# Gate parts requested two steps sooner, a first gate read cut by expert tile, and the last two expert tiles multiplied together

## The chip, the cores and the metric

The kernel runs on one core of a Trainium2 chip. The metric is device time in microseconds (us) of one execution; each version was run several times and the median is what counts.

## The reference

One decoder layer on 512 tokens of 1024 channels: a gated convolution and recurrence mixer, then a product-key expert layer (PEER), then a final norm. The change touches the expert layer and the end only. Cut to what matters there:

```python
q  = (xc @ w_q)                        # 8 heads, two halves
v1, i1 = top_k(s1, 16); v2, i2 = top_k(s2, 16)
top_s, pos = top_k(all pair sums, 16)  # 16 of 128*128 experts per head
g   = softmax(top_s)
act = gelu(sum(u_sel * xc))            # u_sel = expert_u[idx]
out = sum(g * act * v_sel)             # v_sel = expert_v[idx]
h   = h + out
return rms_norm(h, norm_final)
```

## The kernel before

Matrix products are made from a high and a low part of each float32 operand: `split` (lines 72 to 77) writes the high part on ScalarE (ACT, line 75) and the low part on VectorE (DVE) or GpSimd (POOL) (line 76), and three TensorE (PE) matmuls make the product. `weights` (line 79) loads a tile of 512 KB with a DMA on SyncE's queue (SP, line 81) into one of four `raw` buffers and splits it.

The expert layer treats its 512 tokens in two ways. The last 128 are gathered: POOL fetches the chosen experts' rows, DVE multiplies and sums them (`gathered`, line 400). The first 384 (ND, three groups of 128, NT) go through all 128 tiles of 128 experts densely. For this a gate value for each of the 384 tokens and 16384 experts is made by one-hot products (lines 570 to 593), which pass through a staging tile `stg` to a scratch array `gscr` in DRAM: twelve stores of 2 MB, line 593, on ACT's DMA queue. In `gscr` the gates of one expert row, eight tiles (JG) and 32 tokens lie in one piece of 1 KB.

Per tile j, `act_tile` (line 370) multiplies the tokens with the tile's `expert_u` and applies gelu on ACT (line 378). For 76 of the tiles (those in `LAG`) that is done ahead, beside the making of the gates; twelve of them stay on the chip (`keep`), the others are written to `ascr` and read back (`back`, line 674) three steps before use. `out_tile` (line 639) multiplies the activations with the gates on DVE (line 649), splits them into `w_hi` and `w_lo`, and adds three token groups times two column halves into six accumulators `acc` on PE (line 658): 18 matmuls a tile. The loop of line 684 runs one tile ahead: act_tile(j), then out_tile(j-1).

The gates come back from `gscr` in groups of eight tiles, in two buffers `gt`: `read_gates` (line 631). Of each next group four parts, of three token blocks each, are requested in the tiles with k = 3, 4, 5 and 6 of the present group (k = j % 8, lines 645 and 646). The first group is read in six parts of two token blocks at j = 0 (lines 643 and 644). The requests stand on ACT in the order in which the program is written; ACT works through its instructions in order, and a request goes out when ACT comes to it.

At the end, `finish` (line 614) takes each token group's two accumulators: two squares with sums on ACT, an addition, a square root (ACT, line 620), a reciprocal, two multiplications on DVE (line 624), two stores. In the last tile the 18 matmuls go token group by token group, so that the groups become ready one after the other.

Of the kernel before, what the change touches and what calls it, by code (L numbers as in the profile page):

```python
# [11 lines left out]
F32 = mybir.dt.float32  # L12
# [5 lines left out]
AF = mybir.ActivationFunctionType  # L18
# [3 lines left out]
P = 128  # L22
D = 1024
S = 512
# [11 lines left out]
TG = 32  # L36
NG = ND // TG
JG = 8
# [18 lines left out]
def layer(ctx: ExitStack, tc: tile.TileContext, a):  # L57
    nc = tc.nc
    V, A, G, T, SP = nc.vector, nc.scalar, nc.gpsimd, nc.tensor, nc.sync
# [7 lines left out]
    def bank(names, shape=(P, S), dt=F32):  # L67
        i = rot.get(names, 0)
        rot[names] = i + 1
        return ps_pool.tile(list(shape), dt, tag="b" + names[i % len(names)], name="ps")  # L70
# [8 lines left out]
    def weights(src, k, eng=None):  # L79
        raw = ring.tile([P, k * P], F32, tag="raw", name="raw", bufs=4)  # L80
        SP.dma_start(raw, src)
        hi, lo = split(raw, [P, k * P], ("whi", "wlo"), ring, 3, eng)
        return hi.rearrange("p (k m) -> p k m", k=k), lo.rearrange("p (k m) -> p k m", k=k)
# [19 lines left out]
    epst = cst.tile([P, 1], F32, name="epst")  # L103
# [8 lines left out]
    gscr = dram.tile([NG, P, P, TG], F32, name="gscr")  # L112
# [36 lines left out]
    with tc.tile_pool(name="mix", bufs=1) as mp:  # L149
# [9 lines left out]
        for k in range(KD):  # L159
            n = mp.tile([P, S], F32, tag="tmp", name="xg", bufs=3)  # L160
# [8 lines left out]
        for j in range(2, NEARLY):  # L169
            w = weights(a["w_in"][24 + j], KD)  # L170
# [19 lines left out]
        acc = cst.tile([P, KR], F32, name="acc_t")  # L190
# [23 lines left out]
        for j in range(KR):  # L214
# [16 lines left out]
            c = next(columns)  # L231
            held[c] = proj(c, COLS)
            gates = []
            for s, bname, tag in ((0, "brg", "lr"), (1, "big", "lx")):
# [3 lines left out]
                gt = mp.tile([P, S], F32, tag=tag, name=tag, bufs=KR)  # L238
# [88 lines left out]
        for i in range(KD):  # L327
# [4 lines left out]
            n = mp.tile([P, S], F32, tag="tmp", name="hg", bufs=3)  # L332
# [50 lines left out]
    def lag_tiles(n):  # L383
        for _ in range(n):
            j = next(ahead_of_gates, None)
            if j is None:
                return
            kept[j] = act_tile(j)
            if j not in LAG[:JK]:
                A.dma_start(ascr[j], kept[j])  # L390
# [9 lines left out]
    def gathered(i, pin=False):  # L400

        r = gp.tile([P, 2 * D], F32, tag="row", name="row", bufs=4)
        ins = G.indirect_dma_start(  # L403
            out=r, out_offset=None, in_=a["uv"], in_offset=bass.IndirectOffsetOnAxis(ap=uidx[:, i : i + 1], axis=0)
        )
        if pin:
            tc.keep_in_program_order(ins)
        junk = gp.tile([P, D], BF16, tag="junk", name="junk", bufs=1)
        tc.keep_in_program_order(
            V.scalar_tensor_tensor(junk, r[:, :D], 1.0, n2tok, op0=ALU.mult, op1=ALU.mult, accum_out=dots[:, i : i + 1])  # L410
        )
        A.activation(dots[:, i : i + 1], dots[:, i : i + 1], AF.Gelu_apprx_tanh)
        A.activation(dots[:, i : i + 1], dots[:, i : i + 1], AF.Copy, scale=gk[:, i : i + 1])  # L413
        if lastrow:
            gathered_sum()
        lastrow.append((i, r))
# [5 lines left out]
    with tc.tile_pool(name="top", bufs=1) as rp:  # L422
# [77 lines left out]
        for hd in range(H):  # L500
            qs = []
            for s in range(2):
                n = 2 * hd + s
# [48 lines left out]
    with tc.tile_pool(name="gates", bufs=1) as rp:  # L552

        ioR = rp.tile([P, P, 2], F16, name="ioR")
        G.iota(ioR, pattern=[[1, P], [0, 2]], base=0, channel_multiplier=0, allow_small_or_imprecise_dtypes=True)
        TP = TE // 2

        def rows_of(t, t0):
            def bc(x):
                return x[:, t0 : t0 + TE].rearrange("p (q t) -> p q t", t=2).unsqueeze(2).to_broadcast([P, TP, P, 2])  # L560

            e12 = rp.tile([P, 2, TP, P, 2], F16, tag="e12", name="e12", bufs=2)
            ehl = rp.tile([P, 2, TP, P, 2], F16, tag="ehl", name="ehl", bufs=2)
            for s in range(2):
                V.tensor_tensor(e12[:, s], ioR.unsqueeze(1).to_broadcast([P, TP, P, 2]), bc(iT[t][:, s]), op=ALU.is_equal)  # L565
            for s in range(2):
                V.tensor_mul(ehl[:, s], e12[:, 0], bc(gT[t][:, s]))  # L567
            return e12[:, 1], ehl[:, 0], ehl[:, 1]

        blocks = [(t, t0) for t in range(NT) for t0 in range(0, P, TE)]  # L570
        ahead = rows_of(*blocks[0])
        for n, (t, t0) in enumerate(blocks):
            e2, eh, el = ahead
            if n + 1 < len(blocks):
                ahead = rows_of(*blocks[n + 1])
            c, s0 = divmod(t0, TG)
            if s0 == 0:
                stg = rp.tile([P, P, TG], F32, tag="stg", name="stg", bufs=2)
            for q4 in range(TE // 4):
                pg = bank("4567")  # L580
                for i in range(4):
                    o = pg[:, i * P : (i + 1) * P]
                    ti = 4 * q4 + i
                    T.matmul(o, e2[:, ti // 2, :, ti % 2], eh[:, ti // 2, :, ti % 2], start=True, stop=False)
                    T.matmul(o, e2[:, ti // 2, :, ti % 2], el[:, ti // 2, :, ti % 2], start=False, stop=True)
                A.activation(
                    stg[:, :, s0 + 4 * q4 : s0 + 4 * q4 + 4],
                    pg.rearrange("p (t i) -> p i t", t=4),
                    AF.Copy,
                    scale=1.0 / GSC,  # L590
                )
            if s0 + TE == TG:
                A.dma_start(gscr[t * (P // TG) + c], stg)
            left = NL - AR - AD * NT - AT
            lag_tiles((n + 1) * left // len(blocks) - n * left // len(blocks))
            for i in range(n * UP // len(blocks), (n + 1) * UP // len(blocks)):
                gathered(i)
        lag_tiles(AT)


    ep = ctx.enter_context(tc.tile_pool(name="exp", bufs=1))
    gfin = ep.tile([P, D], F32, name="gfin")
    SP.dma_start(gfin, a["nfin"].to_broadcast([P, D]))
    acc = [[ps_pool.tile([P, S], F32, tag=f"b{2 + 2 * t + f}", name=f"acc{t}{f}") for f in range(2)] for t in range(NT)]
    def residual(k):
        hk = ep.tile([P, S], F32, tag="hk", name="hk", bufs=2)
        SP.dma_start(hk, hscr[:, k, :])
        c = (k % 4) * P
        for t in range(NT):
            T.matmul(  # L610
                acc[t][k // 4][:, c : c + P], hk[:, t * P : (t + 1) * P], ident, start=False, stop=False, skip_group_check=True
            )
# [13 lines left out]
                SP.dma_start(a["out"][t * P : (t + 1) * P, fs], o[:, fs])  # L626

    nout = 0
    gst = {}

    def read_gates(n, c0, c1):

        if n * JG >= P:
            return
        if c0 == 0:
            gst[n] = ep.tile([P, NG, JG, TG], F32, tag="gt", name="gt", bufs=2)
        tc.keep_in_program_order(A.dma_start(gst[n][:, c0:c1], gscr[c0:c1, :, n * JG : (n + 1) * JG, :].rearrange("c p j t -> p c j t")))

    def out_tile(j, g):
        nonlocal nout  # L640
        k = j % JG
        if j == 0:
            for c in range(0, NG, 2):
                read_gates(0, c, c + 2)
        if 3 <= k < 7:
            read_gates(j // JG + 1, 3 * k - 9, 3 * k - 6)
        gt = gst[j // JG][:, :, k, :]
        gv = g.rearrange("p (c t) -> p c t", t=TG)
        tc.keep_in_program_order(V.tensor_mul(gv, gv, gt))
        v = weights(a["uv"][j * P : (j + 1) * P, D:], KD, V)  # L650
        vf = [x.rearrange("p k m -> p (k m)") for x in v]
        w = split(g, [P, ND], ("w_hi", "w_lo"), ep, 2)
        passes = [(x, y, f) for x, y in ((0, 0), (0, 1), (1, 0)) for f in range(2)]
        if nout == P - 1:
            passes.sort(key=lambda p: p[2])
        for t in range(NT):
            for x, y, f in passes:
                T.matmul(  # L658
                    acc[t][f],
                    w[x][:, t * P : (t + 1) * P],  # L660
                    vf[y][:, f * S : (f + 1) * S],
                    start=nout == 0 and (x, y) == (0, 0),
                    stop=nout == P - 1 and (x, y) == (1, 0),
                    skip_group_check=True,
                )
        nout += 1

    spilled = list(LAG[JK:])
# [15 lines left out]
    for j in range(P + 1):  # L684
        if j < P:
            read_back(j + PRE)
            g = kept[j] if j in LAG else act_tile(j)
            part += share[j]
        if prev is not None:
            out_tile(*prev)  # L690
        if 8 <= j < 8 + 2 * KD and j % 2 == 0:
            residual(j // 2 - 4)
        prev = (j, g)
        while done < min(len(work), math.ceil(part * len(work) / total)):
            work[done]()
            done += 1
# [54 lines left out]
```

## Time and profile before

| | us |
|---|---|
| median of 3 runs (1783.91 to 1791.77) | 1784.34 |
| the profiled execution, its own time | 1786.26 |
| its span in the profile | 1784.5 |
| PE busy, share of the span | 97% |
| DVE busy, share | 72% |
| ACT busy, share | 43% |

The busy share of PE is an average over stages, and a busy PE is not one at its peak: matmuls are pipelined. More is to be had from the places where PE waits, from the granted clock after such a wait, and from what stands after the last matmul. The dense expert stage, in which PE adds into `acc`, runs from 1011 us to 1776 us.

### The profile page before, as it was taken

To read this page: it belongs to the slowest core of one execution; us is meant where nothing else is said; L and a number is where in the kernel's file an instruction comes from. 1 tells how busy PE (TensorE), PEld (TensorE's weight loads), DVE (VectorE), ACT (ScalarE), POOL (GpSimd) and SP (SyncE) were. 2 spreads that over 40 slices of the span, in tenths; PEclk is the share of its full clock that TensorE was granted. 3 is DMA by queue.
4 is the path that set the end of the run, shared out by engine and by line. 5 is a ranking of instruction groups with operands and counts; after the bars stand their busy time and mean duration, and the time that the engine had idled before them with its cause. 6 is when DMAs were issued, how large, how long until landed. Compare 5 with 4: busy or idle time off the path is not lost.

```text
span 1784.5 us, 23972 instructions
## 1 busy us (share of the span) xinstructions
PE 1728.9 (97%) x8861; PEld 1509.5 (85%) x8861; DVE 1287.8 (72%) x2341; ACT 764.2 (43%) x1290; POOL 325.2 (18%) x257
## 2 busy tenths in 40 slices
PE   7999999999989999899999899999999999999998
PEld 6888888888879888899999788888888887888886
DVE  8979443224578658999998576788777786878774
ACT  5774342222343335455454343444443443444353
POOL 0000000000045555122221121222211222212200
PEclk9999999999999999899999999999999999999999
DMA  4323322332433334579999898999888998999862
GB/s 169 113 81 108 103 77 91 108 102 96 130 112 105 106 113 164 191 275 343 363 368 385 307 332 307 320 339 356 325 297 306 334 339 292 333 338 346 308 237 88
DMA packets 124247, 410.85 MB, mean 230 GB/s; under 512 B 12129, under 2 KB 55393, under 8 KB 106081
## 3 DMA queue, kind: packets, MB, share of 16 engines
q1 hardware_dynamic: 59904, 199.58, 32.8%
q0 software_dynamic: 18432, 134.23, 19.7%
q10 hardware_dynamic: 45792, 75.51, 11.8%
q8 instruction: 69, 1.13, 0.2%
q14 instruction: 50, 0.40, 0.1%
HBM read 367.33 MB, written 41.94 MB: 229 GB/s over the span
## 4 chain that ended last, share of the span: by engine, by line
PE 77%; DVE 11%; DMA 6%; issue 4%; ACT 1%; POOL 1%; SPq 0%; DVEq 0%; POOLq 0%; ACTq 0%
PE ps L90 48%; PE acc L658 26%; DMA gt<-gscr 4%; DVE wlo L76 2%; DVE ehl L567 2%; DVE e L565 1%; DMA row<-uv,uidx 1%; DVE yg L397 1%; DVE junk L410 1%; PE ps L518 1%; PE ps L237 1%; POOL row L403 1%; DMA raw<-ut 1%; DVE nk L142 1%; DMA raw<-w_in 0%
## 5 line engine op out<-in xcount | busy, mean ns | idle before, releaser
L75 ACT ACTIVATE whi<-raw 128x1024 fp32r<-128x1024 f32 (+1 forms) x364 | 380.1, 1046 | 615.0 <-PE ps L90 386.0
L76 DVE TENSOR_TENSOR wlo<-raw,whi 128x1024 fp32r<-128x1024 f32 (+1 forms) x324 | 388.9, 1204 | 263.5 <-ACT whi L75 262.2
L90 PE MATMUL ps<-q_hi,whi 128*128 128x384 f32 (+1 forms) x1232 | 434.4, 353 | 14.9 <-ACT whi L75 10.3
L90 PE MATMUL ps<-q_hi,wlo 128*128 128x384 f32 (+1 forms) x1232 | 429.1, 348 | 2.1 <-DVE wlo L76 2.1
L90 PE MATMUL ps<-q_lo,whi 128*128 128x384 f32 (+1 forms) x1232 | 428.4, 348 | 0.3 <-DVE q_lo L144 0.3
L403 POOL DMA_INDIRECT row<-uv,uidx x128 | 201.4, 1573 | 752.2 <-DVE yg L397 747.6
L658 PE MATMUL acc<-whi,w_hi 128*128 128x512 f32 x768 | 242.4, 396 | 20.6 <-ACT w_hi L75 15.8
L90 PEld LDWEIGHTS ps<-q_hi,whi 128*128 128x128 f32 x1232 | 233.4, 189 | 27.5 <-ACT whi L75 11.6
L90 PEld LDWEIGHTS ps<-q_hi,wlo 128*128 128x128 f32 x1232 | 233.1, 189 | 13.9 <-DVE wlo L76 4.9
L90 PEld LDWEIGHTS ps<-q_lo,whi 128*128 128x128 f32 x1232 | 233.6, 190 | 10.7 <-DVE q_lo L144 0.7
L658 PE MATMUL acc<-wlo,w_hi 128*128 128x512 f32 x768 | 240.7, 394 | 0.0
L658 PE MATMUL acc<-whi,w_lo 128*128 128x512 f32 x768 | 240.7, 394 | 0.0
L658 PEld LDWEIGHTS acc<-whi,w_hi 128*128 128x128 f32 x768 | 145.0, 191 | 50.1 <-ACT w_hi L75 19.0
L658 PEld LDWEIGHTS acc<-whi,w_lo 128*128 128x128 f32 x768 | 146.1, 191 | 31.7 <-DVE w_lo L76 0.7
L658 PEld LDWEIGHTS acc<-wlo,w_hi 128*128 128x128 f32 x768 | 146.0, 190 | 31.5 <-DVE wlo L76 0.3
L90 PE MATMUL ps<-n_hi,whi 128*128 128x512 f32 x432 | 168.5, 390 | 0.0
L90 PE MATMUL ps<-n_hi,wlo 128*128 128x512 f32 x432 | 168.2, 390 | 0.0
L90 PE MATMUL ps<-n_lo,whi 128*128 128x512 f32 x432 | 168.1, 389 | 0.0
L397 DVE SCALAR_TENSOR_TENSOR yg<-row,dots,yg 128x1024 f32<-128x1024 f32 x128 | 164.4, 1284 | 0.8 <-ACT dots L413 0.8
L76 POOL TENSOR_TENSOR wlo<-raw,whi 128x1024 fp32r<-128x1024 f32 x40 | 98.4, 2462 | 357.9 <-ACT whi L75 357.9
L410 DVE SCALAR_TENSOR_TENSOR junk<-row,n2tok 128x1024 bf16<-128x1024 f32 x128 | 156.3, 1221 | 0.2 <-DMA row<-uv,uidx 0.2
L90 PEld LDWEIGHTS ps<-n_hi,wlo 128*128 128x128 f32 x432 | 81.1, 188 | 17.3 <-DVE wlo L76 0.4
(204 smaller groups left out, 1908.1 us busy)
## 6 DMA issues: line engine op xcount, KB each, us to landing
raw<-ut SPq DMA_DIRECT2D x128, 512.0 KB
raw<-uv SPq DMA_DIRECT2D x128, 512.0 KB
raw<-w_in SPq DMA_DIRECT2D x60, 512.0 KB
gscr<-stg ACTq DMA_DIRECT2D x12, 2048.0 KB
gt<-gscr ACTq DMA_DIRECT2D x60, 384.0 KB
ascr<-gel ACTq DMA_DIRECT2D x64, 192.0 KB
back<-ascr ACTq DMA_DIRECT2D x64, 192.0 KB
raw<-w_q SPq DMA_DIRECT2D x16, 512.0 KB
```

The lines of the kernel that those rows point to most:

```text
L75: A.activation(hi, raw, AF.Copy)
L76: (lo_eng or V).tensor_sub(lo, raw, hi.bitcast(F32))
L90: T.matmul(ps, w[x][:, i, :], r[y][i], start=first and n == 0, stop=last and n == 3 * k - 1)
L142: V.scalar_tensor_tensor(n, src[:, k, :], col(gname, k), rstd, op0=ALU.mult, op1=ALU.mult)
L237: T.matmul(pg, x[:, s * P : (s + 1) * P], y, start=n == 0, stop=n == 2)
L397: V.scalar_tensor_tensor(yg, r[:, D:], dots[:, i : i + 1], yg, op0=ALU.mult, op1=ALU.add)
L403: ins = G.indirect_dma_start(out=r, out_offset=None, in_=a["uv"], in_offset=bass.IndirectOffsetOnAxis(ap=uidx[:, i : i + 1], axis=0))
L410: V.scalar_tensor_tensor(junk, r[:, :D], 1.0, n2tok, op0=ALU.mult, op1=ALU.mult, accum_out=dots[:, i : i + 1])
L518: T.matmul(psc[:, s * P : (s + 1) * P], qs[s][:, t * P : (t + 1) * P], keys[:, 2 * hd + s, :], start=True, stop=True)
L565: V.tensor_tensor(e12[:, s], ioR.unsqueeze(1).to_broadcast([P, TP, P, 2]), bc(iT[t][:, s]), op=ALU.is_equal)
L567: V.tensor_mul(ehl[:, s], e12[:, 0], bc(gT[t][:, s]))
L658: T.matmul(acc[t][f], w[x][:, t * P : (t + 1) * P], vf[y][:, f * S : (f + 1) * S], start=nout == 0 and (x, y) == (0, 0), stop=nout == P - ...
```

## The change

Four edits. The four parts of the next group's gates are requested at k = 1 to 4 in place of 3 to 6. The last of the twelve stores is made in two, the first eight tiles' gates and then the rest. The first group's gates are read in three parts cut by tile (0 and 1, 2 and 3, 4 to 7), each over all twelve token blocks, in place of six parts cut by token block. The matmuls of tile 126 are held back until tile 127's operands are there, and then both tiles are multiplied token group by token group; ahead of them a square root on ACT, of which nothing is used, brings the table of that function in.

```diff
             if s0 + TE == TG:
-                A.dma_start(gscr[t * (P // TG) + c], stg)
+
+                for i0, i1 in ((0, P),) if n + 1 < len(blocks) else ((0, JG), (JG, P)):
+                    A.dma_start(gscr[t * (P // TG) + c][:, i0:i1], stg[:, i0:i1])
...
+    operands = []
...
         if j == 0:
-            for c in range(0, NG, 2):
-                read_gates(0, c, c + 2)
-        if 3 <= k < 7:
-            read_gates(j // JG + 1, 3 * k - 9, 3 * k - 6)
+
+            gst[0] = ep.tile([P, NG, JG, TG], F32, tag="gt", name="gt", bufs=2)
+            for j0, j1 in ((0, 2), (2, 4), (4, JG)):
+                tc.keep_in_program_order(
+                    A.dma_start(gst[0][:, :, j0:j1], gscr[:, :, j0:j1, :].rearrange("c p j t -> p c j t"))
+                )
+        if 1 <= k < 5:
+            read_gates(j // JG + 1, 3 * k - 3, 3 * k)
...
-        passes = [(x, y, f) for x, y in ((0, 0), (0, 1), (1, 0)) for f in range(2)]
-        if nout == P - 1:
-            passes.sort(key=lambda p: p[2])
+        operands.append((w, vf))
+        if nout == P - 2:
+            nout += 1
+            return
+
         for t in range(NT):
-            for x, y, f in passes:
-                T.matmul(
...
+            for n, (w, vf) in enumerate(operands):
+                passes = [(x, y, f) for x, y in ((0, 0), (0, 1), (1, 0)) for f in range(2)]
+                last = nout == P - 1 and n == 1
+                if last:
+                    passes.sort(key=lambda p: p[2])
+                for x, y, f in passes:
+                    T.matmul(
...
+        operands.clear()
         nout += 1
...
+        if j == P - 1:
+
+            tc.keep_in_program_order(A.activation(ep.tile([P, 1], F32, name="warm"), epst, AF.Sqrt))
```

The first place is ACT ahead of the boundary to the seventh group (tile 48). Names with a number are buffers; `gt<-gscr` is the request for a part of the gates, `gel<-ps` the gelu of an act_tile, `w_hi` the split of an out_tile, and the words in brackets are the semaphores that are waited for (DMAHW is a DMA that has landed). Before, the fourth part stands between the gelu 11755 and its split, and one tile further comes `w_hi_11839`, the first that needs it:

```order
L378 ACTIVATE gel_11755<-ps_11730 128x384 [waits PE_49]
L637 DMA gt_11575<-gscr_78 128x3x256 [waits DMAHW1_49]
L75 ACTIVATE w_hi_11803<-gel_11755 128x384 [waits DVE_49]
L75 ACTIVATE whi_11865<-raw_11863 128x1024 [waits DMAHW5_49,PE_49]
L412 ACTIVATE dots_3822<-dots_3822 128x1 [waits DVE_49]
L413 ACTIVATE dots_3822<-dots_3822,gk_3821 128x1 [waits Activation_49]
L75 ACTIVATE w_hi_11839<-back_11613 128x384 [waits DMAHW6_49,DVE_49]
```

With the change the same group's fourth part stands here, two tiles ahead of that place:

```order
L378 ACTIVATE gel_11646<-ps_11621 128x384 [waits PE_49]
L640 DMA gt_11506<-gscr_78 128x3x256 [waits DMAHW3_49]
L75 ACTIVATE w_hi_11694<-gel_11646 128x384 [waits DVE_49]
L75 ACTIVATE w_hi_11763<-back_11544 128x384 [waits DMAHW0_49,DVE_49,PE_49]
L75 ACTIVATE whi_11759<-raw_11757 128x1024 [waits DMAHW7_49,PE_49]
```

The request has moved ahead by two tiles' work of ACT; in this group it stands where the third part stood. The three earlier parts have moved with it, and all behind it on ACT keeps its order.

The second place is DVE at the start of the stage, with the change. `keep_3983` is tile 0, `keep_4016` tile 2 and `gel_9403` tile 1:

```order
L656 TENSOR_TENSOR keep_3983<-keep_3983,gt_9405 128x384 [waits DMAHW4_49,DMAHW3_49]
L656 TENSOR_TENSOR keep_4016<-keep_4016,gt_9405 128x384 [waits DMAHW5_49]
L76 TENSOR_TENSOR w_lo_9417<-keep_3983,w_hi_9416 128x384 [waits Activation_49]
L410 SCALAR_TENSOR_TENSOR junk_9440,dots_3822<-row_9438,n2tok_3823 128x1024 [waits DMASW1_49]
L397 SCALAR_TENSOR_TENSOR yg_3824<-row_9365,dots_3822,yg_3824 128x1024
L656 TENSOR_TENSOR gel_9403<-gel_9403,gt_9405 128x384 [waits DMAHW4_49,DMAHW2_49]
```

The order of these is that of before, where the first multiplication waited for all six parts. Now each waits for its own part, and the multiplication of tile 2, with the second part, stands ahead of the low half of tile 0.

The third place is the end of ACT. Before:

```order
L75 ACTIVATE w_hi_15730<-gel_15692 128x384 [waits DVE_49]
L75 ACTIVATE w_hi_15759<-back_15568 128x384 [waits DMAHW3_49,DVE_49,PE_49]
L617 ACTIVATE fo_15781,fss_15783<-acc00_9358 128x512 [waits PE_49]
L617 ACTIVATE fo_15781,fss_15783<-acc01_9359 128x512 [waits PE_49]
L617 ACTIVATE fo_15781,fss_15794<-acc10_9360 128x512 [waits PE_49]
L620 ACT_TABLE_LOAD
L620 ACTIVATE fs1_15786<-fs1_15786,epst_70 128x1 [waits DVE_49]
```

And with the change:

```order
L75 ACTIVATE w_hi_15728<-gel_15690 128x384 [waits DVE_49]
L710 ACT_TABLE_LOAD
L710 ACTIVATE warm_15732<-epst_70 128x1
L75 ACTIVATE w_hi_15741<-back_15566 128x384 [waits DMAHW1_49,DVE_49,PE_49]
L619 ACTIVATE fo_15781,fss_15783<-acc00_9359 128x512 [waits PE_49]
L619 ACTIVATE fo_15781,fss_15783<-acc01_9360 128x512 [waits PE_49]
L622 ACTIVATE fs1_15786<-fs1_15786,epst_70 128x1 [waits DVE_49]
```

The table load has moved ahead of the last tile's split, and each token group's square root now follows its own two squares.

## Rows read from the trace of the kernel before

**Rows 1.** The page, part 4: lines in the chain that ended last.

```profile
PE ps L90 48%; PE acc L658 26%; DMA gt<-gscr 4%; DVE wlo L76 2%; DVE ehl L567 2%; DVE e L565 1%; DMA row<-uv,uidx 1%; DVE yg L397 1%; DVE junk L410 1%; PE ps L518 1%; PE ps L237 1%; POOL row L403 1%; DMA raw<-ut 1%; DVE nk L142 1%; DMA raw<-w_in 0%
```

**Rows 2.** Waits, 1011 us on (us, times, longest); tile gt, idle until.

```profile
PE acc L658 <- ACT w_hi L75: 15.8, 7, 3.7
...
ACT w_hi L75 <- DMA raw<-uv: 0.5, 1, 0.5
...
  DMA gt<-gscr: 34.6, 8
```

**Rows 3.** The chain in order of time: start us, us, what and how many.

```profile
1105.14 6.12 PE acc L658 x18
...
1115.42 4.09 PE acc L658 x18
...
1285.97 9.66 DMA gt<-gscr
1296.82 6.03 PE acc L658 x18
...
1354.72 10.10 PE acc L658 x36
...
1491.74 6.00 PE acc L658 x18
...
1547.38 8.47 PE acc L658 x36
...
1593.83 4.38 PE acc L658 x18
...
1683.76 5.79 PE acc L658 x18
```

**Rows 4.** Windows: length, PE, PEld, DVE, ACT, POOL busy, clock, DMA share, GB/s.

```profile
1296.00:1302.50 6.50, 5.68 (x18) 4.37 (x19) 6.50 (x10) 2.23 (x4) 0.00 (x0) 0.74 0.81 257
1106.00:1286.00 180.00, 180.00 (x870) 158.19 (x869) 143.84 (x185) 75.96 (x140) 41.91 (x27) 0.99 0.91 332
1300.00:1740.00 440.00, 429.46 (x2032) 373.79 (x2032) 336.98 (x435) 185.14 (x335) 84.08 (x58) 0.99 0.87 313
```

**Rows 5.** Timeline, boundary to the seventh group: ACT's requests, then DVE's multiplication.

```profile
1269.98 0.62 ACTq L637 DMA_DIRECT2D gt<-gscr  x1
...
1285.97 0.37 ACTq L637 DMA_DIRECT2D gt<-gscr  x1
...
1295.65 0.56 DVE L649 TENSOR_TENSOR back<-back,gt 128x384 f32<-128x384 f32 x1 [3.58 <-DMA gt<-gscr]
```

**Rows 6.** Start of the stage: ACT, DVE, PE; SP's wait; packets 1003.2:1010, 688:690.5.

```profile
1000.17 0.92 ACTq L637 DMA_DIRECT2D gt<-gscr  x2
...
1010.14 1.03 DVE L649 TENSOR_TENSOR keep<-keep,gt 128x384 f32<-128x384 f32 x2 [1.45 <-DMA gt<-gscr]
...
1011.35 1.19 PE L658 MATMUL acc<-whi,w_hi 128*128 128x512 f32 x2 [4.84 <-issue]
...
SPq L603 <- DMA gscr<-stg: 12.3, 1, 12.3
...
q10 hardware_dynamic: 1632, 1.57, 68.6%
...
q1 hardware_dynamic: 288, 0.13, 19.1%
```

**Rows 7.** The end: PE's last matmul (timeline), then the chain.

```profile
1775.54 0.39 PE L658 MATMUL acc<-whi,w_lo 128*128 128x512 f32 x1
...
1772.56 2.05 ACT fo L617 x6
...
1774.63 1.28 ACT L620
...
1776.22 1.73 ACT fo L617 x6
...
1778.49 1.41 DVE fo L624 x2
```

More of the change, by code (lines that the diff above doesn't have):

```diff
@@ L652, in out_tile @@
         w = split(g, [P, ND], ("w_hi", "w_lo"), ep, 2)
-        passes = [(x, y, f) for x, y in ((0, 0), (0, 1), (1, 0)) for f in range(2)]
-        if nout == P - 1:
-            passes.sort(key=lambda p: p[2])
+        operands.append((w, vf))
+        if nout == P - 2:
+            nout += 1
+            return
         for t in range(NT):
-            for x, y, f in passes:
-                T.matmul(
[L659 to L665, printed above, removed]
+            for n, (w, vf) in enumerate(operands):
[5 more added lines that the diff above has]
+                    T.matmul(
+                        acc[t][f],
+                        w[x][:, t * P : (t + 1) * P],
+                        vf[y][:, f * S : (f + 1) * S],
+                        start=nout == 0 and (x, y) == (0, 0),
+                        stop=last and (x, y) == (1, 0),
+                        skip_group_check=True,
+                    )
+        operands.clear()
         nout += 1
```

## The prediction

> **What bounds the kernel now.** The view to begin with is the chain that ended last. PE leads it, with one stranger of weight: the landing of gate parts, 4% of the span, some 71 us [rows 1]. That share is no gain yet, since PE works through most of each landing. So next come PE's waits from 1011 us on: seven waits for `w_hi`, 15.8 us in all, and almost none of ACT for weights, 0.5 us [rows 2]. `w_hi` is made from the gated activations, and the rows of tile `gt` say what those waited for: DVE stood idle eight times, 34.6 us in all, until gate parts landed [rows 2]. One of the eight is the first group's (below), seven are boundaries between groups.
>
> The timeline at one of them shows why. The second part of four is requested at 1269.98, the fourth at 1285.97, and DVE begins the multiplication at 1295.65, having stood for 3.58 us [rows 5]. A part needs 9.7 us from request to landing, and the fourth is asked for too late by less than that.
>
> Then the price of such a wait, which is more than the wait. In the chain 18 matmuls of a tile take 4.09 us, but 6.12, 6.03 and 6.00 us right after a gap [rows 3]. The window at 1296 has a granted clock of 0.74, against 0.99 in the long stretches [rows 4]: for part of it TensorE ran at 1.2 in place of 2.4 GHz, after PE had stood still.
>
> Is something else ready to take PE's place? In the 180 us from 1106 on there is no gap: PE is busy 180.00 of 180.00, with DMA at 0.91, DVE at 144 and ACT at 76 us [rows 4]. PE sets the pace there. From 1300 to 1740 DMA is at 0.87 and PE lacks 10.5 us [rows 4].
>
> **Part 1, requests two steps sooner.** Removed: the waits at seven boundaries. Idle time, 15.8 us. Slow matmuls, each against 4.09 us for 18 or 8.18 for 36 [rows 3]: 2.03 (1105), 1.94 (1296), 1.92 (1354), 1.91 (1491), 0.29 (1547), 0.29 (1593) and 1.70 (1683), 10.1 us together. Sum 25.9 us. Does two steps suffice? The fourth part now goes out where the second did, in the example 16.0 us sooner, 1269.98 against 1285.97 [rows 5]; DVE's longest wait behind ACT's late request is a few us (34.6 over eight [rows 2]). So none should be left. Added: nothing; the sixty part requests are the same ones, of the same size, at 0.4 to 0.6 us each on ACT's queue. Each reuses the buffer of the group before the present one, whose last multiplication stands two tiles earlier; the order shows no wait of these requests for DVE, only for earlier DMAs, as before. On ACT's DMA queue they pass some `back` reads, which have three steps of lead. With the boundaries gone the same bytes move in 26 us less: 0.87 of 440 is 383 us of DMA work, over some 425 that is 0.90, still under the 0.91 that a gapless stretch carried [rows 4]. I take all of it: **-25.9 us**; bounds 13 (half of the gaps refilled by the next late operand) and 26.
>
> **Part 2, the start.** The store first. SP waited 12.3 us for the last 2 MB store to land, with the weight loads behind it [rows 6]; the tile that SP loads there takes over memory of the staging tile, so it needs both pieces, and the cut doesn't shorten this. The first reads go out at 1000.17, when ACT gets to them, well after that landing. So the store's cut is worth nothing; its second request costs ACT 0.3 us, hidden by ACT's idle half. Then the reads. From the first request to DVE's multiplication 9.97 us pass (1000.17 to 1010.14), and PE stands 4.84 us until 1011.35 [rows 6]. Of the 9.97 the packets themselves take 68.6% of 6.8 us, 4.7 us: 1632 packets over 16 engines, 46 ns each, nearly all of 1 KB. The other 5.3 us are request, queue and weight loads between. The new parts have runs of 256, 256 and 512 bytes, 1536 of them in each part. No row has 256 bytes. The nearest is the stretch at 688: 288 packets, all but 32 of them of 512 bytes, in 19.1% of 2.5 us, 27 ns each [rows 6]. From 46 to 27 ns for half the bytes: the line leads to 18 ns for 256 (an estimate), and 27 is the upper bound by these rows. DVE's second multiplication needs the second part and stands ahead of tile 0's low half, so two parts count: 3072 packets, 3.5 us at 18 ns, 5.2 at 27. With the 5.3 that is 8.8 to 10.5 against 9.97: 1.2 us sooner to 0.5 later. PE gains a bit beside: the first part alone takes 1.7 us, so `w_hi` of tile 0 comes some 3 us sooner, and four matmuls (0.9 us) run before `w_lo` is wanted. I take 18 ns, since the two measured sizes lie on a line: **-2.0 us**, bounds -4 (a wait short enough spares the slow matmuls too) and +1.5.
>
> The Trainium skill ("DMA: Bandwidth & Descriptors", Specifications) has a rule that speaks against this cut: the least transfer for full rate is 512 bytes, and below that the engine reads, modifies and writes. By it part 2 would be the loss of rival (b), and the sum -26 us in place of -30; no row here has such a transfer.
>
> **Part 3, the end.** Before, after the last matmul (1775.93) ACT has ahead of it, the table load having just ended (1774.63 + 1.28): three squares (1.73 us), square roots, then on DVE token group 1's two multiplications (1.41 us) and group 2's [rows 7]. With the change group 0 is complete 24 matmuls (at 4.09 / 18 = 0.23 us each, 5.5 us) and group 1 twelve (2.7 us) before the end, in place of twelve and six; the load is out of the way, and only group 2 is left: one square, 0.68 us (three take 2.05 [rows 7]), an addition, a root, a reciprocal, 1.41 us. Saved: 1.73 - 0.68 = 1.05, one root of 0.3, and 1.41, together 2.8 us. Given back: the load and the idle root stand ahead of the last `w_hi`, which PE now wants six matmuls after tile 126's first; by the timeline's spacing PE may stand 0.2 us, and the addition shows again, 0.2. **-2.3 us**, bounds -1 and -3.
>
> **Sum.** -25.9 - 2.0 - 2.3 = -30.2 us. On the profiled execution's own time, 1786.26, that is 1756; the median of the runs, 1784.34, stands 1.9 lower, so **1754 us**.
>
> **Rivals.** (a) *The weight loads come late.* PE's gaps were also time in which loads caught up; at closed boundaries the next operand is late and half of the 26 us stays. For it: DMA at 0.87 to 0.91, and four more parts in the same few tiles. Against: the gapless 180 us at 0.91, and 0.5 us of waits for weights. Time: 1754 + 13 = 1767. (b) *Small packets cost double*, 36 ns where the line gives 18. Then 3072 of them take 6.9 us, 12.2 us pass in place of 9.97, and the start loses 2 us where I gain 2: 1758. Against: the fall from 46 to 27 ns at half the size. The Trainium skill's rule named in part 2 would bring this about. (c) *Nothing moves*: ACT reaches the earlier requests late, because it stands behind PE's gelu anyhow: 1784. Against: the order has them two tiles ahead, and the second part's time in rows 5. (d) *Slower: ACT stands at the requests.* A request waits for an earlier DMA on its semaphore; two steps sooner that DMA may not have landed, and everything behind on ACT, `whi` and `w_hi`, is late. ACT is busy 76 of 180 us, free 58%, 3.5 us of a 6 us tile. If one request of each of 15 groups stood for a whole landing, 9.7 us, PE would lose 15 x 6.2 = 93 us: about 1847. It outweighs the gain from 2 us over the free time, so from 5.5 us a group. Against: requests at k = 3 to 6 had the same kind of wait, and PE shows none for it.
>
> **Chances.** The forecast 0.75, (a) 0.11, (b) 0.08, (c) 0.03, (d) 0.03. The forecast's own bounds are 1748 to 1763; (b) lies in them, (a) ends at 1767: range **1748 to 1767**, which leaves out part of (a), (c) and (d) and the ends of the bounds. About 0.5% (9 us) is what a measurement of this kernel can tell from no change. Faster by more: forecast, (a) and (b), 0.94. Same: (c), 0.03. Slower: (d), 0.03.
>
> **What would show it.** Right: PE's row for waits on `w_hi` near zero; no idle time of DVE until `gt` beyond the first; a granted clock of 0.99 or 1.0 through the stage; the first `acc` matmul some 3 us sooner, then a short stop; PE's last matmul about 28 us earlier; 6.4 us in place of 8.6 from its end to the end of the span. Wrong: waits of ACT for `raw` (a), the first parts landing after 1010 (b), requests still landing at the boundaries (c), ACT idle at its requests (d).

## The result and the profile after

The changed kernel takes 1755.15 us in the median (four runs, 1753.01 to 1755.78), the kernel before 1784.21 beside it: ratio 0.9824, 95% interval 0.9802 to 0.9846 (it is formed from the runs; the quotient of the two medians is 0.9837). By the medians that is 29.1 us less where 30.2 were forecast; the interval is 27.5 to 35.3 us. Measured again, it took 1756.16 against 1786.56 (ratio 0.9824, 0.9805 to 0.9843), 30.4 us less. The profiled execution took 1753.01 us, its span is 1751.3.

The page's chain, which answers to [rows 1]. The landing of gate parts, 4% before, is no longer in it:

```profile
PE ps L90 49%; PE acc L672 30%; DVE ehl L567 2%; DVE wlo L76 1%; DVE e L565 1%; DMA row<-uv,uidx 1%; PE ps L518 1%; DVE yg L397 1%; DVE junk L410 1%; PE ps L237 1%; DMA gscr<-stg 1%; POOL row L403 1%; DMA raw<-ut 1%; DVE nk L142 1%; DMA raw<-uv 0%
```

Tile `gt` in the trace after, for [rows 2]: DVE's idle time until gate parts landed was 34.6 us in eight stops. Both stops that are left belong to the first group:

```profile
L650 ACTq DMA_DIRECT2D gt<-gscr x3: 380/1129/3538, 999.4 to 1001.0; - x3
...
  DMA gt<-gscr: 5.1, 2
```

PE's waits from 1005 to 1747 us, where before there were 15.8 us for `w_hi`: the answer has its heading and no row. The windows after, for [rows 4] (columns as there):

```profile
1016.00:1747.00 731.00, 729.18 (x3518) 638.62 (x3516) 572.37 (x744) 315.99 (x575) 145.88 (x99) 1.00 0.88 319
1300.00:1740.00 440.00, 440.00 (x2114) 385.69 (x2113) 340.72 (x441) 191.79 (x343) 83.08 (x56) 1.00 0.86 311
1106.00:1286.00 180.00, 180.00 (x872) 157.78 (x871) 142.69 (x184) 77.05 (x141) 40.08 (x26) 1.00 0.92 336
1003.00:1017.00 14.00, 13.85 (x58) 11.45 (x57) 10.24 (x16) 5.58 (x11) 2.02 (x2) 0.90 1.09 304
```

From 1300 to 1740 PE is busy all of 440.00 us, against 429.46, at a granted clock of 1.00. The 180 us that had no gap before are as they were (872 matmuls against 870). The fourth row holds the only stretch in which PE still works at a lower clock, the start of the stage (0.90).

At the boundary to the seventh group, for [rows 5], the timeline has the fourth part's request and DVE's first multiplication with it, 18.4 us later (9.7 before) and without a bracket, so DVE didn't stand for it. The request has moved by 12.3 us and not by the 16.0 of the prediction's example: it stands where the third part stood, as the order ahead of the prediction has it, and the timeline of before has that part, the first line here, at 1273.64, ahead of the fourth at 1285.97. The chain there, for [rows 3], has no tile of over 4.1 us (36 `acc` matmuls, two tiles, in 8.17); it is the third fence.

```profile
1273.64 0.38 ACTq L637 DMA_DIRECT2D gt<-gscr  x1
```

```profile
1264.43 0.38 ACTq L640 DMA_DIRECT2D gt<-gscr  x1
...
1282.78 0.55 DVE L656 TENSOR_TENSOR back<-back,gt 128x384 f32<-128x384 f32 x1
```

```profile
1288.97 4.16 PE ps L90 x24
1293.13 8.17 PE acc L672 x36
1301.30 4.16 PE ps L90 x24
```

The start, for [rows 6], from the timelines of PE, ACT and DVE:

```profile
999.43 1.54 ACTq L650 DMA_DIRECT2D gt<-gscr  x2
...
1000.43 0.44 PE L90 MATMUL ps<-q_hi,whi 128*128 128x384 f32 x1 [2.36 <-ACT whi L75]
...
1001.01 3.54 ACTq L650 DMA_DIRECT2D gt<-gscr  x1
...
1005.58 0.56 DVE L656 TENSOR_TENSOR keep<-keep,gt 128x384 f32<-128x384 f32 x1 [3.95 <-DMA gt<-gscr]
...
1007.17 0.62 PE L672 MATMUL acc<-whi,w_hi 128*128 128x512 f32 x2
1007.32 0.56 DVE L656 TENSOR_TENSOR keep<-keep,gt 128x384 f32<-128x384 f32 x1 [1.18 <-DMA gt<-gscr]
1007.79 0.55 DVE L76 TENSOR_TENSOR w_lo<-keep,w_hi 128x384 fp32r<-128x384 f32 x1
```

From the first request to the first multiplication 6.15 us pass (9.97 before), and the first `acc` matmul follows PE's earlier work with no stop, where it stood 4.84 us. It comes 4.2 us sooner, of which 0.7 are this execution's own: it reached the first request that much earlier (999.43 against 1000.17).

The end, for [rows 7]: PE's last matmul, ACT's table load, which now lies 8.8 us ahead of it, and the last two multiplications:

```profile
1735.97 1.28 ACT L710 ACT_TABLE_LOAD   x1
...
1744.79 0.39 PE L672 MATMUL acc<-whi,w_lo 128*128 128x512 f32 x1
...
1746.66 1.41 DVE L626 SCALAR_TENSOR_TENSOR fo<-acc,fs,gfin 128x512 f32<-128x512 f32 x2
```

From the last matmul's end (1745.18) to the end of the span 6.12 us are left, against 8.57.

### The profile page after: what moved, and what is told of

Its sections match the earlier page's. It is cut to its first block, busy times and chain, and to the rows that moved or that the text cites. A ratio compares the mean times of both kernels' runs of the same rounds, so it can differ in the third digit from the quotient of the medians.

```text
span 1751.3 us, 23967 instructions
## 1 busy us (share of the span) xinstructions
PE 1719.4 (98%) x8861; PEld 1505.5 (86%) x8861; DVE 1287.3 (74%) x2341; ACT 764.2 (44%) x1291; POOL 326.9 (19%) x257
## 3 DMA queue, kind: packets, MB, share of 16 engines
q8 instruction: 69, 1.13, 0.3%
## 4 chain that ended last, share of the span: by engine, by line
PE 81%; DVE 10%; issue 4%; DMA 3%; ACT 1%; POOL 1%; SPq 0%; DVEq 0%; ACTq 0%; POOLq 0%
PE ps L90 49%; PE acc L672 30%; DVE ehl L567 2%; DVE wlo L76 1%; DVE e L565 1%; DMA row<-uv,uidx 1%; PE ps L518 1%; DVE yg L397 1%; DVE junk L410 1%; PE ps L237 1%; DMA gscr<-stg 1%; POOL row L403 1%; DMA raw<-ut 1%; DVE nk L142 1%; DMA raw<-uv 0%
## 5 line engine op out<-in xcount | busy, mean ns | idle before, releaser
L672 PE MATMUL acc<-whi,w_hi 128*128 128x512 f32 x768 | 238.1, 391 | 0.0
```

What stands on the lines that cost most here:

```text
L672: T.matmul(acc[t][f], w[x][:, t * P : (t + 1) * P], vf[y][:, f * S : (f + 1) * S], start=nout == 0 and (x, y) == (0, 0), stop=last and (x, ...
```

## Experiments

Each is the kernel before, or the changed one, with one edit. Differences are of medians, from the kernel before as measured beside each: 1784.88 us under the first heading, 1785.99 under the next two, 1786.56 under the last.

**When the parts are requested**

The requests alone, put into the kernel before:

```diff
-        if 3 <= k < 7:
-            read_gates(j // JG + 1, 3 * k - 9, 3 * k - 6)
+        if 1 <= k < 5:
+            read_gates(j // JG + 1, 3 * k - 3, 3 * k - 0)
```

> The kernel before with one edit: the four parts are requested at k = 1 to 4. My term for this edit is -25.9 us: 1784.2 - 25.9 = 1758. PE's row for waits on w_hi falls from 15.8 us in seven waits to near zero, and no window of the stage after its start has a granted clock under 0.99. Rival 1, the weight loads or another operand are late in the place of the gates and half of the gaps stays: 1771, with a new row of PE or ACT waits of about 13 us. Rival 2, the gain of the whole change came in good part from its other edits (the trace of the changed kernel reaches the stage about 4 us sooner): then this edit gives 20 us or less, 1764 or more.

1761.8 us, 23.1 less (ratio 0.9869, 0.9840 to 0.9899). From 1016 us on PE waits for nothing. The windows from there to the last matmul, of the kernel before and of this one:

```profile
1016.00:1776.00 760.00, 744.17 (x3539) 647.87 (x3538) 571.86 (x738) 315.42 (x570) 144.98 (x99) 0.99 0.85 307
```

```profile
1016.00:1750.00 734.00, 734.00 (x3541) 643.36 (x3540) 571.01 (x738) 314.36 (x569) 146.80 (x99) 1.00 0.87 317
```

The two rows split the gain. Idle time: 760 - 744.17 = 15.8 us. Matmul time: 744.17 / 3539 = 210.3 ns each against 734.00 / 3541 = 207.3, times 3540 is 10.6 us. Together 26 us, the term of 25.9. The profiled executions as a whole agree: 1760.62 against 1786.26, 25.6 less. The medians show 23.1, with an interval of 18.0 to 28.6 us, and can't tell this from 25.9. Of its gain this execution gave a little back in its start: from 1003 to 1017 its granted clock was 0.65, where that of before was 0.88:

```profile
1003.00:1017.00 14.00, 10.16 (x32) 8.59 (x31) 7.86 (x12) 2.98 (x6) 1.01 (x1) 0.65 0.83 266
```

```profile
1003.00:1017.00 14.00, 9.16 (x40) 7.75 (x39) 7.38 (x12) 3.25 (x7) 1.01 (x1) 0.88 0.66 215
```

The first fence is the requests alone, the second the kernel before: eight matmuls fewer in the same 14 us, though PE was busy 1 us more; at 207 ns each that is some 1.7 us. Rival 1 falls, since no new wait came. Rival 2, 20 us or less, falls by the profiled execution's 25.6 and by the next run, in which the other edits alone bring 4.25; the interval of the medians, which begins at 18.0, would not exclude it.

The changed kernel with the requests put back (`if 3 <= k < 7` again):

> The changed kernel with the requests put back to k = 3 to 6, so that only the start and the end are changed. My terms are -2.0 for the start and -2.3 for the end: 1784.2 - 4.3 = 1780, and the seven waits at the boundaries are there again, about 16 us of idle time and about 10 us of matmuls at half the clock. Rival, the start is worth more than I said, since the profile of the changed kernel has its first acc matmul 4.2 us sooner and no slow acc matmul there: 1778 or below. If this kernel and the one with the requests alone do not add up to the whole change (-29.1), the edits are not independent.

1780.63 us (ten runs), 4.25 less than before (0.9978, 0.9962 to 0.9994, which is 1.1 to 6.8 us), the two terms' 4.3. PE's waits for `w_hi` are back, 15.6 us in nine. With the requests alone this makes 27.4 of the whole 29.1 to 30.4: within what these medians can tell, the edits add up.

One step in place of two (`if 2 <= k < 6`), and one step later than before (`if 4 <= k < 8`, in the kernel before):

> The changed kernel with the requests one step sooner than before in place of two, at k = 2 to 5. One step is one tile, 4.1 us of acc matmuls and 4.2 more where the tile's act matmuls lie beside it. DVE's idle time at a boundary was 4.7 us in the mean and PE's 2.3, so my theory expects one step to remove nearly all of PE's waits: at most one or two short ones of under 2 us, 1755 to 1759. Rival, a part lands late because the DMA engines are full and not because it is asked for late: then one step brings half of the gain at most, 1768 or more.

> The kernel before with the requests one step later, at k = 4 to 7. If the lateness of the request sets the wait, the fourth part now goes out in the tile just ahead of the boundary: all 15 boundaries wait, the seven of before for 2.3 + 5.7 = 8 us of PE's time each, the other eight for about 3, which is 80 us in place of 16, and each of the 15 gives about 2 us of slow matmuls, 30 in place of 10: 1784 + 84 = 1868. Rival, PE's queue of finished operands absorbs one step, and only the seven boundaries grow: 7 x 5.7 = 40 us more, 1824. Rival, the landing is set by the DMA load alone: within 10 us of before.

One step sooner gives 1755.44, 29.4 less: all of the gain, so the rival that full DMA engines, and not the request, make the parts late falls. PE's waits from 1006 us on are one, in the start:

```profile
PE acc L672 <- DVE w_lo L76: 1.7, 1, 1.7
```

One step later gives 1825.29, 40.4 more (1.0226, 1.0193 to 1.0260). Its waits, and its window over the stage:

```profile
PE acc L658 <- ACT w_hi L75: 45.2, 12, 7.7
```

```profile
1016.00:1816.00 800.00, 754.78 (x3535) 655.09 (x3534) 572.50 (x739) 315.40 (x569) 140.55 (x100) 0.97 0.82 292
```

Idle time rose by 29.4 us (45.2 against 15.8), matmuls by 754.78 / 3535 - 210.3 = 3.2 ns each, 11 us: 41 in all. So the request's lateness sets the wait, and a wait carries its slow matmuls with it, as the first theory says; but its 84 us was twice too much. The rival's 1824 hit the time by another way than it gave: there are twelve waits, 3.8 us in the mean, at eleven boundaries and not at seven (one boundary has two of them). Why the other four boundaries still don't wait was not tried.

**The start**

The last store in one piece, and the first group read in six parts by token block:

```diff
-                for i0, i1 in ((0, P),) if n + 1 < len(blocks) else ((0, JG), (JG, P)):
-                    A.dma_start(gscr[t * (P // TG) + c][:, i0:i1], stg[:, i0:i1])
+                A.dma_start(gscr[t * (P // TG) + c], stg)
```

> The changed kernel with its last 2 MB store in one piece again. My term for the cut is 0: 1755 within 1.5, with SP's wait for the landing of the store (12.8 us with the cut) as long as there, and the first read's requests at about 999.4 on ACT, when ACT gets to them. Rival, the cut lets the first reads or SP's loads begin sooner: without it the first multiplication of the stage (1005.6 with the cut) is 2 us or more later and the time 1757 or more.

```diff
-            gst[0] = ep.tile([P, NG, JG, TG], F32, tag="gt", name="gt", bufs=2)
-            for j0, j1 in ((0, 2), (2, 4), (4, JG)):
...
+            for c in range(0, NG, 2):
+                read_gates(0, c, c + 2)
```

> The changed kernel with the first group's gates read in six parts by token block, as before. My term for the cut by tile is 2.0 us: 1757, PE with a stop of about 4.8 us ahead of its first acc matmul and slow matmuls behind it. Rival, the cut by tile is worth the whole 4.2 us by which the first acc matmul came sooner, and the half-clock matmuls that follow the long stop besides: 1759 to 1761. Rival by the price of short packets: if packets of 256 bytes were bad, this kernel would be the faster one, 1755 or less.

One store: 1755.91 us, 30.1 less, the same as with two. SP's wait for the landing is 13.1 us (12.8 in two pieces), so the cut is worth nothing. Six parts: 1759.11 us, 26.9 less, where the changed kernel has 29.1 and 30.4, 29.7 in the mean: the cut by tile is worth about 2.8 us, between the term of 2.0 and the rival's 4.2 and more. The interval of this run is 21 to 34 us less, so the medians don't decide between the two; that short packets are bad, with 1755 or less for this kernel, is refuted, its four runs being 1758.38 and more. The stops of PE tell more. For gates and `w_lo` of the first tiles PE stood 4.84, 3.84, 3.31 and 3.31 us in the four profiles with six parts (before, the requests alone, one step later, and this one), 3.8 in the mean. In seven with the cut by tile (the changed kernel, without the requests, one step, one store, the two of the end below, and the changed kernel again) it stood 0, 3.7, 1.7, 1.7, 0.7, 3.1 and 3.1 us, 2.0 in the mean: 1.8 less. The stop in this run:

```profile
1016.22 1.19 PE L669 MATMUL acc<-whi,w_hi 128*128 128x512 f32 x2 [3.31 <-issue]
```

The price of the short packets, from the changed kernel's DMA view of 1002 to 1005 us (queue: packets, MB, share of 16 engines):

```profile
q10 hardware_dynamic: 2431, 0.62, 108.8%
```

0.62 MB over 2431 packets is 255 bytes each; 108.8% of 3 us on 16 engines is 52.2 us, 21 ns a packet (a share of over 100% means that the packets' times overlap). The prediction took 18, with 27 as its upper end.

**The end**

Without the idle square root, and without holding tile 126 back:

```diff
-            tc.keep_in_program_order(A.activation(ep.tile([P, 1], F32, name="warm"), epst, AF.Sqrt))
+            pass
```

> The changed kernel without the idle square root, so that ACT brings the table in at the first group's own square root. The load (1.28 us) then begins when the first group's squares are done, 4.7 us ahead of PE's last matmul, and delays the second group's squares by some 0.4 us, which the pause of 0.8 us ahead of the third group's absorbs: last matmul to end of span 6.1 us as with it, 1755 within 1.5. Rival, the load lies on the path to the end: 1.3 us more, 1756.5, and 7.4 us from the last matmul to the end.

```diff
-        if nout == P - 2:
-            nout += 1
-            return
...
-                last = nout == P - 1 and n == 1
+                last = nout == P - 1
```

> The changed kernel with tile 126 multiplied by itself and tile 127 token group by token group behind it, as before; the idle square root stays. The groups are then ready 2.7 and 1.4 us ahead of the end in place of 5.5 and 2.7. ACT needs 1.35 us for a group's squares and 0.3 for its root, so the second group's squares run past the end of PE by about 1 us: 7.2 us from the last matmul to the end of the span in place of 6.1, 1756.3. Rival, holding the tile back costs PE as much as it gives (a stop ahead of the last two tiles): 1755 or less.

Without the idle root: 1755.64 us, 6.11 us from the last matmul to the end: nothing lost. The timeline of ACT shows the load falling into the pause between two token groups; the third group's squares still had to wait for PE:

```profile
1740.09 1.28 ACT L622 ACT_TABLE_LOAD   x1
...
1744.15 0.60 ACT L619 ACTIVATE fo<-acc 128x512 f32<-128x512 f32 x1 [0.43 <-PE acc L672]
```

Without the hold: 1758.61 us, and 7.35 us after the last matmul (1749.95 of 1757.3), where 7.2 were expected. The tail is thus 8.57 with neither edit, 7.35 with the root alone, 6.11 with the hold alone and 6.12 with both: once the tile is held back, the idle root is worth nothing. The tail explains 1.2 of the 2.3 us by which this kernel's gain, 27.4, is smaller than the changed kernel's 29.7 in the mean; these medians can't place the rest. In this execution PE also stands 1.29 and 1.83 us at the start, but so it does (1.84 and 1.27) in the second profile of the changed kernel.

**More from the start**

In the changed kernel's profile SP's weight loads stand behind `gfin`, whose memory waits for the last store, and PE stands 2.36 us. Four kernels, measured side by side, asked whether that, or the first reads, can give more.

```diff
-    SP.dma_start(gfin, a["nfin"].to_broadcast([P, D]))
...
-        SP.dma_start(hk, hscr[:, k, :])
+        tc.keep_in_program_order(SP.dma_start(hk, hscr[:, k, :]))
...
+        if j == 24:
+            tc.keep_in_program_order(SP.dma_start(gfin, a["nfin"].to_broadcast([P, D])))
```

> The changed kernel with SP's load of the norm weights (gfin) moved from the start of the expert stage to tile 24, and the loads of hk kept in their order behind it, so that SP's weight loads no longer stand behind a tile that waits for the last store. In the profile of the changed kernel PE stands 2.36 and 0.64 us at 1000 us for weights and then runs 3.41 us at half the clock, 1.7 us lost: 4.7 us in all. My theory: the loads go out some 4 us sooner and these go, but the first gates then become late, since ACT comes to their requests only 2 to 3 us sooner; a stop of PE ahead of its first acc matmul of about 2.5 us takes their place: 2 us gained, 1753. Rival 1, the whole 4.7 us are gained: 1750.5. Rival 2, the loads are bounded by the freeing of raw and not by the store: 1755.

> The changed kernel itself, beside the three others of this call, as their measure: 1755 within 1.5.

The changed kernel again: 1756.16 (1751.94 to 1757.04). `gfin` late: 1754.56 (ratios 0.9824 and 0.9820; intervals from 0.9803 to 0.9843 overlap). No wait of SP for the last store is left, but PE's stop for weights is 0.97 us with `gfin` late and also in the second profile of the changed kernel. In six other profiles with this start it is 1.6 to 2.9 us, so one profile of each can't tell what `gfin` gave. What shows is the gates: the second part lands at 1011.65, tile 0's low half stands behind it on DVE, and PE waits there:

```profile
1012.73 1.22 PE L671 MATMUL acc<-whi,w_lo 128*128 128x512 f32 x2 [3.64 <-DVE w_lo L76]
```

So gates do come late in the place of weights, as the theory's later half says, though by 3.64 us where it said 2.5; its price of the loads is not shown. Rival 2, that the loads are bounded by the freeing of `raw`, gave the nearest time, 1755. A gain of 2 us is neither shown nor excluded. The other two write the first requests ahead of the loop; the second also has `gfin` late:

```diff
+    gst[0] = ep.tile([P, NG, JG, TG], F32, tag="gt", name="gt", bufs=2)
+    for j0, j1 in ((0, 2), (2, 4), (4, JG)):
+        tc.keep_in_program_order(
+            A.dma_start(gst[0][:, :, j0:j1], gscr[:, :, j0:j1, :].rearrange("c p j t -> p c j t"))
+        )
```

> The changed kernel with the first group's three requests written ahead of the loop over the tiles, so that on ACT they stand ahead of the first tile's whi and gelu; DVE's order at the start then has tile 0's low half ahead of tile 2's multiplication. SP's loads stay where they are. Theory: the first multiplication comes 2 to 3 us sooner and PE's small stop for w_lo (0.3 to 1.7 us in the runs so far) goes, but the stop of 2.36 + 0.64 us for weights and the half clock after it stay: about 1 us gained, 1754. Rival, the requests wait on ACT for an earlier DMA and hold the work behind them: 1758 or more.

> Both edits: gfin at tile 24 and the first requests ahead of the loop. Theory: neither weights nor gates are late at the start of the stage, PE has no gap of over 1 us between 960 us and its last matmul, and no half-clock window there: 4.7 us of weights and clock and up to 1 us for w_lo, 1750. Rival, only one of the two sums shows, since PE then waits for the next operand of the start: 1753.

1758.57 and 1757.04 us, where the theories said 1754 and 1750: no gain, and the reads alone 2.4 us above the changed kernel measured beside them. The hold that the rival spoke of is in ACT's timeline of the reads alone: the three requests take ACT's queue for 7.01 us, and ACT stands 7.53 ahead of the gelu behind them. The rows show the requests long in being issued; that they wait for an earlier DMA, as the rival had it, is not shown.

```profile
996.48 7.01 ACTq L679 DMA_DIRECT2D gt<-gscr  x3
1003.54 0.49 ACT L378 ACTIVATE gel<-ps 128x384 f32<-128x384 f32 x1 [7.53 <-DMA gt<-gscr]
...
1005.72 1.20 PE L665 MATMUL acc<-whi,w_hi 128*128 128x512 f32 x2 [8.89 <-issue]
```

The edit moved PE's order as well: the 24 matmuls of an `act_tile`, which filled PE's time ahead of the first `acc` matmul, now come behind it, and PE stands 8.89 us. What each of the two costs was not separated. None of the variants is shown to beat the changed kernel.

## Why the prediction was right

**Part 1, -25.9.** The stage shows 15.8 us of idle time and 10.6 of slow matmuls removed, 26 in all. That there would be no new bound held: no wait of PE is left in 742 us. The DMA share from 1300 to 1740 is 0.86 where 0.90 was expected, but this window now ends 5 us ahead of the last matmul, when the loads are over; from 1300 to 1700 it is 0.92, where it was 0.89. So the stage bears a little more than the 0.91 that the prediction relied on. ACT's waits for `raw` from 1007 us on are 1.5 us in two. Rivals (a), (c) and (d) fall by that. The prediction asked whether two steps suffice; one does already, and the second is a margin that costs nothing. Its example was misread (12.3 us of lead gained and not 16.0), which changes nothing, DVE's stop there having been 3.58 us.

**Part 2, -2.0.** The stops of PE give 1.8 us in the mean. The medians give about 2.8 by the six parts (29.7 - 26.9), 1.8 by the changed start and end without the requests (4.25 less the tail's 2.45) and 3.5 by the requests alone (29.1 - 23.1 - 2.45), each with an interval of several us; the term lies among them, and they can't size it more closely. The store's cut was worth nothing, as forecast. The landing was near its terms: the multiplication with the second part began 7.9 us after the first request in the first profile and 9.9 in the second (8.4 to 10.1 in the five others with this cut), where 8.8 to 10.5 were forecast. In most of them that is hardly sooner than the 9.97 of before. The gain is rather what the prediction put beside it: PE begins on the first part, after 6.15 us, and what it then stands, 2.0 us in the mean, is less than the 3.8 with six parts. Rival (b), 36 ns a packet, falls by the 21 ns measured. The Trainium skill's rule ("DMA: Bandwidth & Descriptors", Specifications) that transfers under 512 bytes miss the full rate and are read, modified and written did not show as a doubled price in these reads. A byte did cost more: 255 bytes took 21 ns, where 512 took 27 and 1 KB 46.

**Part 3, -2.3.** 2.45 measured. The working counted the table load's new place beside the hold; the runs show that the hold alone brings all of it. The working's 2.8 less 0.2 and 0.2 is 2.4 and not 2.3.

**The sum.** -30.2 against 29.1 and 30.4. That it fits to 1 us is in part luck, the intervals being some 7 us wide. The forecast's own bounds, 1748 to 1763, are not what its terms' bounds add up to: a gain of 12.5 to 33 us, 1751 to 1772. The profiled execution gained 33.3 us on its counterpart, 1786.26, more than the medians; the stage's start is where executions of one kernel differ. In the changed kernel's second profile PE stood only 0.97 us for weights at 1000 us, and then 1.84 and 1.27 us for gates and `w_lo`, and the slow stretch fell on `acc` matmuls: granted clock 0.76 from 1003 to 1017, against 0.90 in the first profile. That the long stop for weights of the first profile cost little, since it and the slow matmuls behind it lay in time in which the gates were awaited anyhow, fits these rows but was not tested.

## What to carry to other kernels

Before a request is moved ahead, read how long its consumer stands and compare it with one step of the loop; one more step than that is margin. Price a stop of PE with the slow matmuls that follow it: here they were two thirds as much again (10.6 on 15.8 us), and with the longer stops of one step later two fifths (11 on 29 us more). And where several late operands meet, as in the start, removing one wait shows the next: moving three requests ahead held ACT's queue and brought no gain.

## What the runs showed of the hardware that was not expected

Requests of many short runs, one behind the other, hold the queue that issues them: the three first reads of the changed kernel (1536 runs each) took 0.38, 1.13 and 3.54 us on ACT's queue, and 7.01 us together in the kernel with the reads alone, while a group's part (384 runs of 1 KB) took 0.38 in the median. In the changed kernel ACT had nothing else to do in that time; ahead of a gelu the same hold made ACT stand for 7.53 us.

One step of lateness did not cost one step at each boundary: 40.4 us over 15 boundaries is 2.7 us each, slow matmuls included, where a tile's matmuls take 4.1 to 8.2.
